# Two PSUM banks for the last token tile of the last product, and buffers of their own for an early weight tile and the last transposed tile

## The chip, the core and the metric

The kernel runs on one core of one Trainium2 chip. The metric is the device time of one execution in microseconds (us), lower is better. All inputs and the output lie in the chip's memory; nothing is kept from one execution to the next.

The engines named below are TensorE (PE: matmuls, and PEld: its weight loads), VectorE (DVE), ScalarE (ACT), GpSimd (POOL) and SyncE (SP), which here issues nearly all DMA transfers, one after the other in the order of its program.

## The reference

One post-norm encoder layer over 1024 tokens of width 1024, in fp32:

```python
x = layer_norm(ALPHA * x + hybrid_mixer(x) , ln1_g, ln1_b)      # gated spatial unit and mLSTM, then @ w_out
x = layer_norm(ALPHA * x + conv_glu_ffn(x), ln2_g, ln2_b)

def conv_glu_ffn(x, w_up, conv_w, conv_b, w_down):               # D_FF = 2816
    gate, up = split(x @ w_up)
    gate = gelu(causal_dwconv(gate, conv_w, conv_b))             # width 3
    return (gate * up) @ w_down
```

The mixer takes the first third of the time, and the change does not touch its work. The feed-forward part (`conv_glu_ffn`) and the two layer norms around it are what the text is about.

## The kernel before

**Arithmetic.** Every fp32 operand is split into a high part and a remainder (`split_hi`, L74, a cast on ACT; `split_lo`, L77, a subtraction on DVE), and every product is three matmuls (`mm3`, L304 to L306: high by high, then the two mixed ones). The split weights live in a ring of five slots, `WH0` to `WH4` and `WL0` to `WL4`; one slot holds two elements of 128x512. A slot is filled again once the matmuls that read it are done (`done_elem`, `prep`).

**The FFN's first half.** It works on 22 gate/up pairs `p`, each as seven block products (j = 0 to 6) of a Strassen-like scheme. Elements 0 and 1 of a pair are its raw gate tile, elements 2 to 5 are sums that DVE forms (`sums`, L152 to L155), element 6 is raw again. The raw tiles come into the buffer `RW` by `load_up` (L147), one DMA of 512 KB for each half, `w_up[p, 0]` to columns 0 to 1023 and `w_up[p, 1]` to the rest. Elements 0 and 1 of the first three pairs (`first_products`) need only the first half of the tokens and are done ahead, while the mixer's last stage still runs.

**The hand-over from mixer to FFN.** The out-projection goes over eight token tiles t = 0 to 7 (`proj`, matmul L701). For each tile DVE adds the residual (L801) and takes the statistics (L713), centres (L729), and scales (L731, the last step of LN1); SP stores the tile to memory (L803, `x1d`); PE transposes it (`x1T`, L748), ACT copies the transposed halves from PSUM (L749) back over the tile in `acc[t]`, and DVE forms operand sums from it (L760 to L763). `XOP` and `TX` name the resulting operands. Tile 7 is the last; the FFN's operands for the second half of the tokens need it.

**The FFN's second half** (`down_all`) is again a set of seven products, P2, P1, P5, P6, P3, P7, P4 in that order, each of 11 chunks `c` and, for each chunk, four token tiles. Chunk c of the j-th product is step s = 11 j + c, so the last product P4 has s = 66 to 76. Its weight operands are also prepared through the ring (`prep_t`: a load L174, a subtraction L194, and the split). The result of a product and token tile is collected in one bank of PSUM, TensorE's output memory (`A`, four banks named `mm` in the trace; `C`, four named `sm`). `take` (L925, L927) adds a bank to the output tile `acc`.

**What orders the work.** The order of the instructions on each engine is set by a scheduler when the program is built, from the order of the code and the dependences, except in the last product: `down_end` is written under `manual_schedule`, so its order is that of the code. There, before, chunks 0 to 2 of P4 are done for all four token tiles (`HEAD = 3`), then chunks 3 to 10 for tile 0, 1 and 2 of the second half one after the other (acc 4, 5, 6), and then for the last one (acc 7) in two halves of 256 columns. Both halves lie in the same bank, `C[3]`. Behind each, DVE adds (L987; L998 for the last tile's halves) and takes statistics, and `centre`, `affine` (L939, L940) do LN2.

Of the kernel before, what the change touches and what calls it, by code (L numbers as in the profile page):

```python
# [35 lines left out]
def hybrid_encoder_layer(ctx, tc, xT, x, w_qk, w_vg, w_au, w_av, w_o, w_out, w_up, w_down,  # L36
# [100 lines left out]

    def raw_of(p, j, n=1):
        if j in (0, 1):
            return RW[:, j * 512:(j + n) * 512]  # L140
        if j == 6:
            return RW[:, 1536:2048]
        return AP_[0][:, (j - 2) * 512:(j - 2 + n) * 512]
# [10 lines left out]
        nc.vector.tensor_tensor(s3, a11, a21, op=ALU.subtract)  # L154
        nc.vector.tensor_tensor(s4, a12, s2, op=ALU.subtract)  # L155

    def runs(s):

        if s >= 7 * NC:
            return []  # L160
        if s == 7 * NC - 1:
            return [(s, 1)]
        return [(s, 2)] if s // NC == (s + 1) // NC else [(s, 1), (s + 1, 1)]


# [10 lines left out]
    def prep_t(s, n):  # L176

        nonlocal ntr
        name, c = PRODS[s // NC], s % NC
        ch = chain[0][:, c * 512:(c + n) * 512] if chain else None  # L180
        if name == "P1":
            raw = ch
        else:
            raw = TR[ntr % 4][:, 0:n * 512]
            ntr += 1
        load_t(raw.rearrange("p (c d) -> p c d", c=n), name, c, n)
        if name in ("P5", "P6", "P7", "P4"):
            if name in ("P5", "P6"):
                nc.vector.tensor_tensor(ch, raw, ch, op=ALU.subtract)
                raw = ch  # L190
            elif name == "P7":
                nc.vector.tensor_tensor(raw, ch, raw, op=ALU.subtract)
            else:
                nc.vector.tensor_tensor(raw, raw, ch, op=ALU.subtract)  # L194
        split(E1 + s, raw, n)

    chain = []

# [5 lines left out]
    def prep(e):  # L204

        if e >= E1:
            for s, n in runs(e - E1):
                prep_t(s, n)
            return
        i = e - E0  # L210
        two = SEQ[i:i + 2]
        if i == 0:
            load_up(0)
        if two[0][0] == two[1][0] and two[0][1] in (0, 2, 3, 4):
            p, j = two[0]
            if j == 2 and p > 0:
                sums(p)
            split(e, raw_of(p, j, 2), 2)
            if j == 0 and 0 < p < EARLY - 1:
                load_up(p + 1, (0,))  # L220
            return
        for q, (p, j) in enumerate(two):
            if j == 2 and p > 0:
                sums(p)
            split(e + q, raw_of(p, j))
            if j == 6 and p + 1 < NF:
                load_up(p + 1)
# [512 lines left out]
    def x1T(t):  # L740

        ts_ = slice((t % 4) * P, (t % 4 + 1) * P)
        a3 = acc[t].rearrange("p (k t) -> p k t", k=NK)
        for g in range(2):
            pt = smps()
            for i in range(4):
                k = g * 4 + i
                nc.tensor.transpose(pt[:, i * P:(i + 1) * P], acc[t][:, k * P:(k + 1) * P], ident)  # L748
            nc.scalar.copy(acc[t][:, g * 512:(g + 1) * 512], pt)  # L749

        def put(xh, xl, src):
            split_hi(xh[:, :, ts_], src)
            split_lo(xl[:, :, ts_], src, xh[:, :, ts_])

        if t < 4:
            put(XH[0], XL[0], a3)
            return
        b3 = acc[t - 4].rearrange("p (k t) -> p k t", k=NK)
        t3 = tmp.tile([P, 512], F32, name="t2", bufs=4).rearrange("p (k t) -> p k t", k=4)
        nc.vector.tensor_tensor(t3, a3[:, 4:8, :], a3[:, 0:4, :], op=ALU.subtract)  # L760
        nc.vector.tensor_tensor(a3[:, 0:4, :], a3[:, 0:4, :], b3[:, 0:4, :], op=ALU.subtract)
        nc.vector.tensor_tensor(b3[:, 0:4, :], a3[:, 4:8, :], a3[:, 0:4, :], op=ALU.subtract)
        nc.vector.tensor_tensor(b3[:, 4:8, :], b3[:, 4:8, :], b3[:, 0:4, :], op=ALU.subtract)  # L763
        late_puts["TX"].append(lambda: put(*TX24, b3))
        late_puts["X1"].append(lambda: put(XH[1], XL[1], a3))
        late_puts["T3"].append(lambda: put(*XOP["T3"], t3))
# [7 lines left out]
    for t in range(NT):  # L774
        nc.sync.dma_start(acc[t], x[t * P:(t + 1) * P, :])
        pss = [mmps(), mmps()]
        if t == NT - 1:
            sums(0)
            load_up(1, (0,))
        proj(t, ys, pss, range(4))  # L780
        nys = prep_y(t + 1) if t < NT - 1 else None
        if t == NT - 2:
            mctx.close()
            fctx = ExitStack()
            ffn = fctx.enter_context(tc.tile_pool(name="ffn", bufs=1, reuse_waits="tile"))
            TX24 = [ffn.tile([P, NK, 512], F32R, name=f"TX{i}") for i in range(2)]
            GR2 = ffn.tile([P, 1032], F32, name="GR2")
            XOP.update(T2=[w[:, 0:4, :] for w in TX24], T4=[w[:, 4:8, :] for w in TX24],
                       T3=(JJ.rearrange("p (k t) -> p k t", k=4), T3L))
        if t >= NT - 2:  # L790
            puts("TX")
        proj(t, ys, pss, (4, 5))
        if t >= 1:
            x1T(t - 1)
        if t >= NT - 2:
            puts("TX")
        proj(t, ys, pss, (6, 7))
        ys = nys
        for g in range(2):
            a = acc[t][:, g * 512:(g + 1) * 512]  # L800
            nc.vector.scalar_tensor_tensor(a, a, ALPHA, pss[g], op0=ALU.mult, op1=ALU.add)  # L801
        ln_dve(acc[t], lng, moments(stats(acc[t], HALVES)))
        nc.sync.dma_start(x1d[t], acc[t])  # L803
# [82 lines left out]
    def load_s(s0):  # L886

        nonlocal nsr
        for s, n in runs(s0):
            raw = SR[nsr % len(SR)][:, 0:n * 512].rearrange("p (c t) -> p c t", c=n)  # L890
            nsr += 1
            nc.sync.dma_start(raw, sd[s // NC, s % NC:s % NC + n].rearrange("c p t -> p c t"))
            sh, sl = s_slot(s, n)
            split_hi(sh, raw)
            split_lo(sl, raw, sh)

    def step(j, c, bank, t, first, cols=slice(0, 512)):
        s, tail = j * NC + c, j == len(PRODS) - 1
        th, tl = elem(E1 + s)
        sh, sl = (w[:, 0, t * P:(t + 1) * P] for w in s_slot(s, 1))  # L900
        mm3(bank[:, cols], sh, sl, th[:, cols], tl[:, cols], first and c == 0, c == NC - 1 or tail and c == HEAD - 1,
            not first or tail and c >= HEAD)

    def done_step(j, c):
        s = j * NC + c
        done_elem(E1 + s)
        if s % 2 == 1:
            load_s(s + 15)

    HEAD = 3  # L910

    def down_product(name, bank, first, between=None):
        j = PRODS.index(name)
        for c in range(NC if name != "P4" else HEAD):
            if c == 4 and between:
                between()
            for t in range(4):
                step(j, c, bank[t], t, first)
            done_step(j, c)

# [54 lines left out]
    def down_end(A, C):  # L975
        j = PRODS.index("P4")
        take(A, 1, 1, False)
        down_product("P4", C, True)
        half_stats(1, 1)
        take(A, 1, 0, True)  # L980
        for t in range(3):
            for c in range(HEAD, NC):
                step(j, c, C[t], t, True)
            if t == 2:
                affine(5, nc.gpsimd, nc.sync)
            a = acc[4 + t][:, 0:512]
            nc.vector.tensor_tensor(a, a, C[t], op=ALU.add)  # L987
            nc.vector.bn_stats(LS[:, 4 + t, 0, :], a)
            centre(4 + t)
            if t == 1:  # L990
                affine(4, nc.gpsimd, nc.sync)
        t, a = NT - 1, acc[NT - 1]
        for i, cols in enumerate((slice(0, 256), slice(256, 512))):
            for c in range(HEAD, NC):
                step(j, c, C[3], 3, True, cols)
            if i == 0:
                affine(6, nc.vector, nc.sync)
            nc.vector.tensor_tensor(a[:, cols], a[:, cols], C[3][:, cols], op=ALU.add)  # L998
            nc.vector.bn_stats(LS[:, t, 2 * i, :], a[:, cols])
        mv = moments_of(t, 3)  # L1000
        rs = rstd_of(mv[:, 1:2], 1)
        nc.vector.scalar_tensor_tensor(a, a, mv[:, 0:1], lng[0], op0=ALU.subtract, op1=ALU.mult)
        for (lo, hi), q in zip(((0, 512), (512, 1024)), (nc.scalar, nc.sync)):
            nc.vector.scalar_tensor_tensor(a[:, lo:hi], a[:, lo:hi], rs, lng[1][:, lo:hi], op0=ALU.mult, op1=ALU.add)
            q.dma_start(out[t * P:(t + 1) * P, lo:hi], a[:, lo:hi])
# [83 lines left out]
```

## Time and profile before

| what | value |
|---|---|
| time, median of 3 runs | 1035.51 us (1035.13 to 1036.37) |
| the profiled execution: its own time | 1035.04 us |
| its span on the engines | 1033.2 us |
| mean granted clock of TensorE | 0.993 of full speed |
| busy: PE / PEld | 1013.2 us (98%) / 827.9 us (80%) |
| busy: DVE / ACT / POOL | 695.7 us (67%) / 428.6 us (41%) / 72.2 us (7%) |

The span runs from the first to the last instruction that the profiler saw; the profiled execution's own time is 1.84 us more (1035.04 - 1033.2). All times of rows below are counted from the start of the span. Busy shares are means over the span: what a wait costs has to be read where it is.

### The profile page before, as it was taken

Reading aid. Unit: us, or ns where it says so; the run is one execution under the profiler, and the core shown is the slowest. Engines: PE = TensorE matmul, PEld = TensorE weight load, DVE = VectorE, ACT = ScalarE, POOL = GpSimd, SP = SyncE. Lnnn points to the kernel's source line nnn. Section 1 sums busy time; section 2 is a strip of 40 time slices with the busy share of each in tenths; the row PEclk is TensorE's granted clock in tenths of the full one; section 3 lists DMA queues with packets and bytes.
Section 4 is the critical chain, followed back from the end, with each engine's and each line's share of the span. In section 5 each row is a group of like instructions: output and inputs, shape, how many; then the busy total and the mean of one; then the engine's idle time right before and its main releaser. Section 6 shows DMA issues by size and latency. Waiting matters only on the chain.

```text
span 1033.2 us, 12796 instructions
## 1 busy us (share of the span) xinstructions
PE 1013.2 (98%) x4769; PEld 827.9 (80%) x4769; DVE 695.7 (67%) x1187; ACT 428.6 (41%) x659; POOL 72.2 (7%) x84
## 2 busy tenths in 40 slices
PE   9999999999999989999999999999999999999994
PEld 7899777888888867888888888888888888888884
DVE  7432346775566789877776776776776688466885
ACT  6533666342222245443343443443345453333410
POOL 0000112222100000000000000000000000000512
PEclk9999999999999999999999999999999999999997
DMA  8122420333111142332322322322346998256312
GB/s 291 61 71 82 124 82 22 114 111 102 62 62 42 41 158 90 131 111 82 130 95 82 126 99 82 122 102 82 119 168 223 318 311 284 104 174 203 133 51 82
DMA packets 60254, 127.32 MB, mean 123 GB/s; under 512 B 6624, under 2 KB 8992, under 8 KB 60192
## 3 DMA queue, kind: packets, MB, share of 16 engines
q1 hardware_dynamic: 60048, 126.24, 36.3%
q8 instruction: 37, 0.61, 0.2%
q10 hardware_dynamic: 144, 0.26, 0.1%
q14 instruction: 25, 0.20, 0.1%
HBM read 97.88 MB, written 28.61 MB: 122 GB/s over the span
## 4 chain that ended last, share of the span: by engine, by line
PE 60%; DVE 3%; DMA 0%; POOL 0%; ACT 0%; issue 0%; POOLq 0%; DVEq 0%
PE mm L305 15%; PE mm L306 15%; PE mm L304 15%; PE sm L304 6%; PE sm L306 6%; PE sm L305 6%; DMA RW<-in_w_up_dram 0%; DVE WL L77 0%; DVE ACC L939 0%; DVE ACC L731 0%; ACT ACC L734 0%; POOL rs L296 0%; POOL ACC L940 0%; POOLq L1085 0%; DVE t L760 0%
## 5 line engine op out<-in xcount | busy, mean ns | idle before, releaser
L304 PE MATMUL mm<-XH,WH 128*128 128x512 f32 x392 | 156.2, 398 | 3.0 <-ACT WH L74 2.5
L305 PE MATMUL mm<-XL,WH 128*128 128x512 f32 x392 | 155.0, 395 | 1.0 <-DVE XL L77 1.0
L306 PE MATMUL mm<-XH,WL 128*128 128x512 f32 x392 | 155.4, 397 | 0.0
L77 DVE TENSOR_TENSOR WL<-RW,WH 128x512 fp32r<-128x512 f32 (+3 forms) x115 | 95.1, 834 | 52.8 <-ACT WH L74 51.2
L74 ACT CAST WH<-RW 128x512 fp32r<-128x512 f32 (+3 forms) x115 | 79.7, 699 | 122.0 <-PE mm L305 55.1
L304 PEld LDWEIGHTS mm<-XH,WH 128*128 128x128 f32 x392 | 74.1, 189 | 21.3 <-ACT WH L74 3.5
L305 PEld LDWEIGHTS mm<-XL,WH 128*128 128x128 f32 x392 | 74.1, 189 | 18.9 <-DVE XL L77 2.0
L306 PEld LDWEIGHTS mm<-XH,WL 128*128 128x128 f32 x392 | 73.9, 188 | 18.0 <-DVE WL L77 1.1
L296 POOL TENSOR_TENSOR rs<-ve,negh 128x4 f32<-128x4 f32 (+1 forms) x32 | 29.4, 922 | 765.0 <-DVE ve L294 762.0
L304 PE MATMUL sm<-WH,XH 128*128 128x512 f32 (+1 forms) x184 | 71.9, 391 | 6.6 <-DVE ACC L998 6.6
L347 PE MATMUL mm<-WH,XH 128*128 128x260 f32 (+1 forms) x256 | 77.3, 342 | 0.0
L347 PE MATMUL mm<-WH,XL 128*128 128x260 f32 (+1 forms) x256 | 76.2, 338 | 0.0
L347 PE MATMUL mm<-WL,XH 128*128 128x260 f32 (+1 forms) x256 | 76.1, 338 | 0.0
L74 ACT CAST XH<-SR 128x1024 fp32r<-128x1024 f32 (+1 forms) x38 | 36.8, 971 | 89.7 <-PE mm L305 45.8
L74 ACT CAST WH<-AP 128x1024 fp32r<-128x1024 f32 (+1 forms) x55 | 48.2, 879 | 58.4 <-PE mm L305 25.8
L305 PE MATMUL sm<-WL,XH 128*128 128x512 f32 (+1 forms) x184 | 71.7, 390 | 0.0
L306 PE MATMUL sm<-WH,XL 128*128 128x512 f32 (+1 forms) x184 | 71.6, 389 | 0.0
L304 PE MATMUL mm<-TX,WH 128*128 128x512 f32 x176 | 69.4, 394 | 0.0
L305 PE MATMUL mm<-TX,WH 128*128 128x512 f32 x176 | 69.3, 394 | 0.0
L306 PE MATMUL mm<-TX,WL 128*128 128x512 f32 x176 | 69.2, 393 | 0.0
L77 DVE TENSOR_TENSOR XL<-SR,XH 128x1024 fp32r<-128x1024 f32 (+1 forms) x38 | 44.6, 1180 | 34.0 <-ACT XH L74 33.9
L77 DVE TENSOR_TENSOR WL<-AP,WH 128x1024 fp32r<-128x1024 f32 (+1 forms) x55 | 55.3, 1007 | 5.6 <-ACT WH L74 4.6
(273 smaller groups left out, 2043.5 us busy)
## 6 DMA issues: line engine op xcount, KB each, us to landing
RW<-in_w_up_dram SPq DMA_DIRECT2D x46, 512.0 KB, 3.4
SR<-sd SPq DMA_DIRECT2D x31, 512.0 KB, 4.2
sd<-ACC SPq DMA_DIRECT2D x44, 256.0 KB, 3.1
S<-in_w_down_dram SPq DMA_DIRECT2D x15, 512.0 KB, 4.7
RW<-in_w_down_dram SPq DMA_DIRECT2D x15, 512.0 KB, 4.6
sd<-t SPq DMA_DIRECT2D x22, 256.0 KB, 2.6
RW<-in_w_out_dram SPq DMA_DIRECT2D x16, 256.0 KB, 3.2
S<-in_xT_dram SPq DMA_DIRECT2D x12, 256.0 KB, 5.5
```

Source lines behind the costliest of these rows:

```text
L74: nc.scalar.copy(hi, src)
L77: nc.vector.tensor_tensor(lo, src, hi.bitcast(F32), op=ALU.subtract)
L296: nc.gpsimd.tensor_tensor(rs, ve, negh[:, 0:n], op=ALU.pow)
L304: nc.tensor.matmul(ps, lh, rh, start=first, stop=False, skip_group_check=more)
L305: nc.tensor.matmul(ps, lh, rl, start=False, stop=False, skip_group_check=more)
L306: nc.tensor.matmul(ps, ll, rh, start=False, stop=last, skip_group_check=more)
L347: nc.tensor.matmul(pss[g][:, 0:width], lhs[:, k, :], rhs[:, k % 2, g * width:(g + 1) * width], start=(k == 0 and i == 0), stop=(k == NK - ...
```

## The change

It has four parts. (1) The early gate tile of pair 1 is loaded to a buffer of its own, `late[3]` (named S3), and `RW` takes pair 2's at once; before, pair 2's was loaded after pair 1's had been split. (2) The transposed last tile is written to `lng[0]` (named S9), not back over `acc[7]`. (3) The operand of the very last step, s = 76, has a place of its own in `JJ`, and is prepared at the end of P7. (4) In P4, chunks 0 and 1 (`HEAD = 2`) are done for three token tiles; the last token tile comes alone afterwards with all 11 chunks, its second half in another bank (`mmps()`), and `affine(6)` on DVE stands behind the first half's add.

```diff
     def raw_of(p, j, n=1):
         if j in (0, 1):
-            return RW[:, j * 512:(j + n) * 512]
+            return (late[3] if p == 1 else RW)[:, j * 512:(j + n) * 512]
...
-    def runs(s):
+    def runs(s, left=False):
...
         if s == 7 * NC - 1:
-            return [(s, 1)]
+            return [(s, 1)] if left else []
...
-        split(E1 + s, raw, n)
+        wh, wl = t_op(s, n)
+        split_hi(wh, raw)
+        split_lo(wl, raw, wh)
+
+    def t_op(s, n=1):
+        return (JJ[:, 0:512], JJ[:, 512:1024]) if s == 7 * NC - 1 else elem(E1 + s, n)
...
             split(e, raw_of(p, j, 2), 2)
-            if j == 0 and 0 < p < EARLY - 1:
-                load_up(p + 1, (0,))
...
-        a3 = acc[t].rearrange("p (k t) -> p k t", k=NK)
+        raw = acc[t] if t < NT - 1 else lng[0]
+        a3 = raw.rearrange("p (k t) -> p k t", k=NK)
...
-            nc.scalar.copy(acc[t][:, g * 512:(g + 1) * 512], pt)
+            nc.scalar.copy(raw[:, g * 512:(g + 1) * 512], pt)
...
         if t == NT - 1:
+            nc.sync.dma_start(late[3][:, 0:1024], w_up[1, 0])
             sums(0)
-            load_up(1, (0,))
+            load_up(2, (0,))
...
-        s, tail = j * NC + c, j == len(PRODS) - 1
-        th, tl = elem(E1 + s)
+        s = j * NC + c
+        th, tl = t_op(s)
...
         done_elem(E1 + s)
+        if s == 6 * NC - 1:
+            prep_t(7 * NC - 1, 1)
...
-    HEAD = 3
+    HEAD = 2
...
-            for t in range(4):
+            for t in range(4 if name != "P4" else 3):
                 step(j, c, bank[t], t, first)
...
-        for i, cols in enumerate((slice(0, 256), slice(256, 512))):
-            for c in range(HEAD, NC):
-                step(j, c, C[3], 3, True, cols)
-            if i == 0:
+        for i, (cols, bank) in enumerate(((slice(0, 256), C[3]), (slice(256, 512), mmps()))):
+            for c in range(NC):
+                step(j, c, bank, 3, True, cols)
+            if i == 1:
                 affine(6, nc.vector, nc.sync)
-            nc.vector.tensor_tensor(a[:, cols], a[:, cols], C[3][:, cols], op=ALU.add)
+            nc.vector.tensor_tensor(a[:, cols], a[:, cols], bank[:, cols], op=ALU.add)
```

`load_up(1)`, later in the program, is unchanged and brings `w_up[1, 0]` to `RW` once more, although `S3` holds it.

In the orders below a row is one instruction: its line, its operation, what it writes, what it reads, and the size; "x2" is two in a row. SP's queue at the hand-over, before (RW is the weight buffer, x1d the store of an LN1 tile, ACC4 to ACC7 the tiles 4 to 7, S9 and S10 buffers for the second half's weights):

```order
L803 DMA x1d_945<-ACC4_83 128x1024
L803 DMA x1d_945<-ACC5_84 128x1024
L803 DMA x1d_945<-ACC6_85 128x1024
L147 DMA RW_80<-in_w_up_dram 128x1024 x2
L174 DMA S9_89<-in_w_down_dram 128x2x512
L147 DMA RW_80<-in_w_up_dram 128x1024
L803 DMA x1d_945<-ACC7_86 128x1024
L174 DMA S10_90<-in_w_down_dram 128x2x512
L147 DMA RW_80<-in_w_up_dram 128x1024 x4
```

The same place of SP's queue after the change:

```order
L808 DMA x1d_945<-ACC4_83 128x1024
L782 DMA S3_88<-in_w_up_dram 128x1024
L808 DMA x1d_945<-ACC5_84 128x1024
L808 DMA x1d_945<-ACC6_85 128x1024
L147 DMA RW_80<-in_w_up_dram 128x1024 x3
L808 DMA x1d_945<-ACC7_86 128x1024
L174 DMA S10_90<-in_w_down_dram 128x2x512
L147 DMA RW_80<-in_w_up_dram 128x1024
L174 DMA S9_89<-in_w_down_dram 128x2x512
L147 DMA RW_80<-in_w_up_dram 128x1024 x2
```

One load more stands there, S3's; the two of RW behind the store of ACC6 have become three (pair 2's gate tile, pair 1's again, pair 2's again), the S9 load has moved behind the store of ACC7, and the second half of pair 1 (the single RW load) is now behind that store and S10's load, where before it was ahead of the store.

DVE around the start of the last product, before (RW, S10 hold raw operands of the last product, `chain` the matrix that is subtracted, WL2 to WL4 ring slots, ACC4 to ACC7 the output tiles):

```order
L194 TENSOR_TENSOR RW_80<-RW_80,chain_6144 128x1024
L77 TENSOR_TENSOR WL2_77<-S10_90,WH2_72 128x1024
L927 TENSOR_TENSOR ACC4_83<-ACC4_83,mm_6165 128x512
L927 TENSOR_TENSOR ACC5_84<-ACC5_84,mm_6166 128x512
L927 TENSOR_TENSOR ACC6_85<-ACC6_85,mm_6167 128x512
L927 TENSOR_TENSOR ACC7_86<-ACC7_86,mm_6168 128x512
L194 TENSOR_TENSOR RW_80<-RW_80,chain_6144 128x512
L77 TENSOR_TENSOR WL3_78<-RW_80,WH3_73 128x1024
L77 TENSOR_TENSOR WL4_79<-RW_80,WH4_74 128x512
L931 BN_STATS LS_6147<-ACC4_83 128x6
```

The same place after the change (JJ holds the operand of step 76):

```order
L194 TENSOR_TENSOR RW_80<-RW_80,chain_6144 128x1024
L194 TENSOR_TENSOR RW_80<-RW_80,chain_6144 128x512
L77 TENSOR_TENSOR WL2_77<-S10_90,WH2_72 128x1024
L77 TENSOR_TENSOR JJ_87<-RW_80,JJ_87 128x512
L933 TENSOR_TENSOR ACC4_83<-ACC4_83,mm_6165 128x512
L933 TENSOR_TENSOR ACC5_84<-ACC5_84,mm_6166 128x512
L933 TENSOR_TENSOR ACC6_85<-ACC6_85,mm_6167 128x512
L933 TENSOR_TENSOR ACC7_86<-ACC7_86,mm_6168 128x512
L937 BN_STATS LS_6147<-ACC4_83 128x6
L77 TENSOR_TENSOR WL3_78<-RW_80,WH3_73 128x1024
L937 BN_STATS LS_6147<-ACC5_84 128x6
```

The subtraction and the split of step 76 (128x512) have moved ahead of the four adds, and the split of steps 74 and 75 (WL3) now has one statistics instruction more ahead of it.

DVE at the end, before (ACC6 and ACC7 are the last two output tiles, LN0 and LN1 the gain and bias of LN2, sm_7294 the bank of the last tile):

```order
L939 TENSOR_TENSOR ACC6_85<-ACC6_85,LN0_6145 128x1024
L940 TENSOR_TENSOR ACC6_85<-ACC6_85,LN1_6146 128x1024
L998 TENSOR_TENSOR ACC7_86<-ACC7_86,sm_7294 128x256
L999 BN_STATS LS_6147<-ACC7_86 128x6
L998 TENSOR_TENSOR ACC7_86<-ACC7_86,sm_7294 128x256
```

And after, where the last tile's halves are in sm_7298 and mm_7451:

```order
L1004 TENSOR_TENSOR ACC7_86<-ACC7_86,sm_7298 128x256
L1005 BN_STATS LS_6147<-ACC7_86 128x6
L945 TENSOR_TENSOR ACC6_85<-ACC6_85,LN0_6145 128x1024
L946 TENSOR_TENSOR ACC6_85<-ACC6_85,LN1_6146 128x1024
L1004 TENSOR_TENSOR ACC7_86<-ACC7_86,mm_7451 128x256
```

The first half's add and statistics have moved ahead of tile 6's gain and bias, and the second half's add reads another bank.

## Rows read from the trace of the kernel before

**Rows 1.** The page's first line.
```profile
span 1033.2 us, 12796 instructions
```

**Rows 2.** Waits of PE: line, what it waited for, total us, times, longest.
```profile
PE sm L304 <- DVE ACC L998: 6.6, 1, 6.6
```

**Rows 3.** Windows: us, busy time (count) by engine, granted clock, DMA share, GB/s.
```profile
377.00:377.50 0.50, 0.50 (x1) 0.48 (x2) 0.50 (x1) 0.50 (x1) 0.00 (x0) 0.50 0.56 184
389.00:389.50 0.50, 0.00 (x0) 0.00 (x0) 0.50 (x2) 0.50 (x2) 0.00 (x0) 1.00 0.00 0
440.00:980.00 540.00, 540.00 (x2333) 437.69 (x2332) 389.67 (x508) 229.20 (x304) 12.83 (x7) 1.00 0.44 150
```

**Rows 4.** PE's timeline at the hand-over: start, us, instruction, idle before and releaser.
```profile
376.98 0.79 PE L304 MATMUL mm<-XH,WH 128*128 128x512 f32 x1 [2.12 <-ACT WH L74]
...
380.47 0.39 PE L305 MATMUL mm<-XL,WH 128*128 128x512 f32 x1
...
382.39 1.06 PE L748 MATMUL sm<-ident,ACC 128*128 128x128 f32 x8 [0.59 <-DVE ACC L731]
...
389.53 0.49 PE L304 MATMUL mm<-XH,WH 128*128 128x512 f32 x1 [0.54 <-ACT XH L74]
390.80 0.50 PE L305 MATMUL mm<-XL,WH 128*128 128x512 f32 x1 [0.77 <-DVE XL L77]
...
393.74 0.49 PE L305 MATMUL mm<-TX,WH 128*128 128x512 f32 x1
```

**Rows 5.** ACT's timeline at the hand-over.
```profile
375.89 1.04 ACT L74 CAST WH<-RW 128x1024 fp32r<-128x1024 f32 x1 [2.87 <-DMA RW<-in_w_up_dram]
...
385.31 1.07 ACT L749 COPY ACC<-sm 128x512 f32<-128x512 f32 x2 [2.84 <-DMA x1d<-ACC]
...
389.39 0.61 ACT L74 CAST WH<-RW 128x512 fp32r<-128x512 f32 x1
```

**Rows 6.** DVE's timeline at the hand-over.
```profile
361.94 1.28 DVE L731 SCALAR_TENSOR_TENSOR ACC<-ACC,rs,S 128x1024 f32<-128x1024 f32 x1 [0.43 <-POOL rs L296]
...
369.62 1.23 DVE L77 TENSOR_TENSOR WL<-RW,WH 128x1024 fp32r<-128x1024 f32 x1
...
380.96 1.28 DVE L731 SCALAR_TENSOR_TENSOR ACC<-ACC,rs,S 128x1024 f32<-128x1024 f32 x1 [0.44 <-POOL ACC L811]
```

**Rows 7.** SP's queue at the hand-over, two loads of RW in one row.
```profile
364.45 6.76 SPq L147 DMA_DIRECT2D RW<-in_w_up_dram  x2
```

**Rows 8.** The tile RW from 340 to 420 us: its DMAs from issue to landing.
```profile
DMA to landing us min/median/max: 3.2/3.4/5.0
```

**Rows 9.** PE's timeline in the last product.
```profile
985.75 0.40 PE L304 MATMUL sm<-WH,XH 128*128 128x512 f32 x1
...
1010.80 0.28 PE L304 MATMUL sm<-WH,XH 128*128 128x256 f32 x1
...
1020.35 0.58 PE L304 MATMUL sm<-WH,XH 128*128 128x256 f32 x1 [6.56 <-DVE ACC L998]
```

**Rows 10.** DVE's timeline in the last product.
```profile
988.00 1.21 DVE L194 TENSOR_TENSOR RW<-RW,chain 128x1024 f32<-128x1024 f32 x1
...
990.47 2.47 DVE L927 TENSOR_TENSOR ACC<-ACC,mm 128x512 f32<-128x512 f32 x4
992.87 0.68 DVE L194 TENSOR_TENSOR RW<-RW,chain 128x512 f32<-128x512 f32 x1
...
1005.43 0.69 DVE L987 TENSOR_TENSOR ACC<-ACC,sm 128x512 f32<-128x512 f32 x1 [2.67 <-PE sm L306]
...
1017.47 1.23 DVE L939 TENSOR_TENSOR ACC<-ACC,LN 128x1024 f32<-128x1024 f32 x1 [1.31 <-ACT ACC L734]
...
1025.78 0.42 DVE L998 TENSOR_TENSOR ACC<-ACC,sm 128x256 f32<-128x256 f32 x1 [5.03 <-PE sm L306]
```

**Rows 11.** SP's queue at the end: the load of step 76's operand.
```profile
984.58 0.37 SPq L174 DMA_DIRECT2D RW<-in_w_down_dram  x1
```

**Rows 12.** DMA issues from 960 us on: engine, operation, KB each, median us to landing.
```profile
RW<-in_w_down_dram SPq DMA_DIRECT2D x1, 256.0 KB, 3.6
```

More of the change, by code (lines that the diff above doesn't have):

```diff
@@ L888, in load_s @@
         nonlocal nsr
-        for s, n in runs(s0):
+        for s, n in runs(s0, True):
             raw = SR[nsr % len(SR)][:, 0:n * 512].rearrange("p (c t) -> p c t", c=n)
@@ L897, in step @@
     def step(j, c, bank, t, first, cols=slice(0, 512)):
-        s, tail = j * NC + c, j == len(PRODS) - 1
-        th, tl = elem(E1 + s)
+        s = j * NC + c
+        th, tl = t_op(s)
         sh, sl = (w[:, 0, t * P:(t + 1) * P] for w in s_slot(s, 1))
-        mm3(bank[:, cols], sh, sl, th[:, cols], tl[:, cols], first and c == 0, c == NC - 1 or tail and c == HEAD - 1,
-            not first or tail and c >= HEAD)
+        mm3(bank[:, cols], sh, sl, th[:, cols], tl[:, cols], first and c == 0, c == NC - 1, not first)
     def done_step(j, c):
```

## The prediction, made before the changed kernel was run

> **What bounds the kernel now.** First the busy times by engine (the table above): PE is busy for 1013.2 of the 1033.2 us [rows 1], so a gain has to come from the 20 us in which it waits or from time in which it runs slowly. Then PE's waits, of which the largest is one of 6.6 us for DVE's add at L998 [rows 2]. Then the windows: from 440 to 980 us PE is busy for all 540.00 us at the full clock [rows 3], so nothing that only hastens another engine there is worth anything, and what is gained ahead of it is carried unchanged to the end. The two places to look at are the hand-over, 360 to 394 us, and the last product, from 985.75 us on.
>
> At the **hand-over** PE waits 2.12 us until 376.98 for an ACT cast of RW, and that cast starts at 375.89, when a load of RW has landed [rows 4, 5]. This is pair 2's gate tile: its load is the second of SP's row that starts at 364.45, held back until DVE's split of pair 1 at 369.62 has ended, 370.85 [rows 6, 7]. Behind the wait PE's clock is half: 0.50 in the window at 377 us against 1.00 later [rows 3], the lower of its two levels, 1.2 against 2.4 GHz. The seven starts from 376.98 to 380.47 take 3.49 us; at full clock a matmul of 512 columns takes 0.232 us in a row ((1010.80 - 985.75) / 108 matmuls between the two [rows 9]), so 1.62, and 1.87 are lost. Three short waits follow: 0.59 for tile 7's LN1 scale on DVE, then 0.54 and 0.77 for its operands [rows 4]. In all 2.12 + 1.87 + 0.59 + 0.54 + 0.77 = 5.89 us.
>
> In the **last product** the last tile's first half ends at 1020.35 - 6.56 = 1013.79, and PE does not start the second before DVE has added the first, because both are in one bank [rows 9]. DVE does not come to that add because tile 6's gain and bias (L939 at 1017.47, L940 after it) stand ahead, and they wait for ACT's normalising of tile 6 [rows 10]. The second half's add then comes at 1025.78, after 5.03 us of idle DVE, and 7.42 us of tail follow up to 1033.2.
>
> **The end, part by part.** The matmuls are as many as before: 36 + 72 of 512 columns and 24 + 24 halves against 18 + 81 and 33 + 33, 132 times 512 columns either way. What moves:
>
> (a) The second half has its own bank and follows the first at once. Its bank is one of the four that P7 used and DVE's second `take` empties; that is done about 1000, 14 us before it is wanted, so I cost it at nothing.
>
> (b) On DVE the 76-step's subtraction (0.60, a half-width instruction like the one at 992.87 [rows 10], less the 0.08 by which neighbours overlap) and its split (0.60) now stand ahead of WL2 and of the four adds, and WL3's split comes after the adds and one statistics instruction. From 988.00: subtraction 1.13, step 76's 0.60, WL2 1.14, JJ 0.60, four adds 2.40 (2.47 in a row [rows 10]), statistics 0.60, and WL3 1.22 gives 995.7. PE wants WL3 (steps 74 and 75) with the 38th matmul: tile 0 now follows after 18 matmuls of the head, not 36, and 18 more for its chunks 2 to 7, and one with the high part: 985.75 + 37 x 0.232 = 994.3. So a new wait of about 1.4. Before, 36 + 15 + 1 matmuls stood ahead, PE came to it at 997.8, and there was no wait. Below nothing it cannot be; above, it grows with any lateness of DVE.
>
> (c) The load of step 76's operand (issued at 984.58 [rows 11], 3.6 to land [rows 12]) is there at 988.2, and DVE comes to it at 989.1. It is hidden by 0.9; beyond that each us of lateness goes to PE.
>
> (d) Where that 1.4 is found again. Tile 0's end is hidden, since DVE is busy with the adds till about 1000. Tile 1 ends after 18 + 54 matmuls and the wait, 985.75 + 72 x 0.232 + 1.4 = 1003.9, and DVE's add of it starts about 1004.0; before, it started at 1005.43, after 36 + 48 = 84 matmuls and a wait for PE [rows 10]. So this add comes about 1.35 earlier. The chain behind it on DVE and ACT, 12.04 us from 1005.43 to L939's start for tile 6 at 1017.47 [rows 10], is the same instructions and bounded by their own durations: L939 of tile 6 at 1016.1. The first half's add now stands before it, in the idle 1.31 there (PE ends that half about 1014.2: 99 x 0.232 + 33 x 0.116 + 1.4 behind 985.75 is 1013.9, and the add about 1014.8). L939 and L940 take 2.4, so DVE is free for the second half's add at 1018.5. PE ends that half at 1013.9 + 33 x 0.116 = 1017.7 to 1018.1. The add at 1018.53 instead of 1025.78: a gain of **7.25**, with DVE, not PE, last. Without the wait in (b) the whole chain is 1.35 earlier still, but PE then needs 1016.7: 8.6 at most.
>
> **The hand-over.** Pair 1's gate tile is now loaded to S3 behind the store of tile 4, ahead of the loads of RW, and its split no longer has to wait for the sums of pair 0, nor to end before RW is loaded again. RW's load of pair 2 is issued once DVE has formed the sums of pair 0 and is landed by 371.6 even at the longest landing of 5.0 [rows 8]; the split is done by 373. PE wants it at 374.86. So the wait of 2.12 and the slow clock behind it, 3.99, go.
>
> What is late next is tile 7's LN1 on DVE. Two splits now stand ahead of tile 6's scale (361.94 [rows 6]), which waits 0.43 there: 361.94 + 2 x 1.14 - 0.43 = 363.8. From it to tile 7's there are, in the new order, ten instructions of half width at 0.60, five splits or centrings at 1.14 to 1.2, tile 6's own 1.2 and a small one, 13.2: about 377.2, against 380.96 before, where DVE too sat idle for the missing cast. The transposes follow 1.4 behind, about 378.6. PE, without its wait, is there at 382.39 - 0.59 - 3.99 = 377.8. A new wait of 0.8, then, and tile 7's transposes 3.8 earlier. ACT's copies of them no longer wait for the store of tile 7: before they waited 2.84 for it [rows 5], and PE was 0.54 and 0.77 late behind them [rows 4]; those 1.31 go as well. PE alone would be 3.8 + 1.31, with the early matmul below 5.4, earlier.
>
> But the other half of pair 1 (`w_up[1, 1]`) now stands in SP's queue behind the store of tile 7 and S10's load, and waits for the split of pair 0's last element, done about 382. It lands 3.2 to 5.0 later [rows 8]; with the 3.4 of the median and a little for the neighbours, at 385.7. ACT's cast of it and, behind it, three more (0.61 + 1.04 + 1.04 + 0.61 [rows 5], 3.2 with their overlaps), and DVE's sums, are queued behind that landing; with 0.3 from the last cast to PE, the matmul that stood at 393.74 [rows 4] comes 3.5 after it, at 389.2. One matmul of its group is done ahead of it, so the gain is 393.74 - 389.2 + 0.23 = **4.8**. With a landing in 5.0 it is 3.4 (387.1 instead of 385.7); it cannot be above 5.4.
>
> The load that brings `w_up[1, 0]` a second time, and pair 2's tile after it, lie in SP's queue ahead of tile 7's store and are through by 376.4, before the store can go at 378.6; they cost nothing as long as that cover of 2 us holds. The DMA engines are busy for 0.56 of the window at 377 us, with 184 GB/s [rows 3]. The Trainium skill (DMA: Bandwidth & Descriptors, "Issuing engines are not separate DMA queues") says that all transfers end on the same 16 engines and interleave; by that rule the three added or moved 512 KB loads lengthen each other, and the gain is the 3.4, the time 1024.9. Nothing in the median of the landings speaks for that, so the sum stays with 4.8.
>
> **Sum.** 1035.04 - 7.25 - 4.8 = 1023.0 for an execution like the profiled one. Its 1035.04 is 0.47 below the median of the runs, 1035.51, so I predict 1023.5, a gain of 12.0, or 1.2%. A difference within 0.2% (2.1 us) is about what a measurement of this kernel can't tell from none.
>
> **The rivals.**
> - *Hand-over gain given back.* The moved load of `w_up[1, 1]` lands late, or DVE's order makes tile 7's scale later than 377.2; the gain there is 1 to 3. For it: three loads and a store follow each other closely. Against: landings were 5.0 at most [rows 8]. Time 1025.3 to 1027.3. Chance 0.2.
> - *The clock falls in a new wait.* In the 2.12 us wait it fell, and 1.87 were lost in the matmuls after it [rows 4]; across the waits of 0.54 and 0.77, close together, it stayed at 1.00 [rows 3]. The new waits, 0.8 at the transposes and 1.4 in the last product, lie between. If it falls once, about 1.9 more: 1025.4. Chance 0.14. The Trainium skill (TensorE: Matmul & The Clock Gate, "A second HAM failure mode: psum-queue depth-cycling") reports that short idles between groups of matmuls let the clock swing; by that rule a fall is likelier than I make it.
> - *The second bank does not help*, because its emptying is late or DVE's order still holds PE. The end then keeps its 6.6 wait: 1035.5 - 4.8 = 1030.7. Chance 0.02.
> - *Slower than before.* DVE's new subtraction waits for step 76's load; DVE and then PE stand behind it. To undo 12.0 us it must be 12.9 later than 988.2, so land 16.5 us after issue, where 3.6 was measured [rows 12]. Chance 0.02; a landing that leaves the time the same (13 to 16 us), 0.02.
> - The forecast, 1021.5 to 1024.7: 0.6.
>
> **How the numbers follow.** The low end is 7.25 + 1.35 for no wait at WL3, with 5.4 at the hand-over: 1035.51 - 14.0 = 1021.5. The high end is both gains short: 7.25 - 1.9 for a fallen clock and 3.2: 1027.0. Faster by over 0.2% is all but the last cases, 0.96.
>
> **What the changed profile should show.** No wait of 6.6 us in the last tile; PE without gaps there. A wait of about 1.4 us on a DVE split about 8.5 us after the last product starts. The last half's add about 7 us nearer to the product's start, right behind L946, with 7.4 of tail. At the hand-over no wait for a cast of RW at pair 2's first element and a clock of 1.00 after it; the transposes of tile 7 some 3.8 us earlier, behind a wait of under 1 us for the scale; one wait of under 1.5 us at the first sums of pair 1, for ACT or DVE behind the load. From there to the last product everything earlier by 4.8. Wrong would be: a clock of 0.50 behind one of the new waits; WL3's wait absent or above 2; the load of `w_up[1, 1]` landing after 386.5; or PE, not DVE, last at the second half's add.

## The result and the profile after

The changed kernel takes 1022.91 us (median of 4 runs, 1022.7 to 1023.92) against 1035.32 for the kernel before in the same comparison (4 runs, 1034.93 to 1036.37): a ratio of 0.9881, 95% interval 0.9863 to 0.9898. 1023.5 was predicted. The profiled execution of after took 1022.7 us, its span is 1020.9, 12.3 less than before [rows 1].

The page's first lines of after, the span and the busy times by engine:

```profile
span 1020.9 us, 12811 instructions
...
PE 1008.1 (99%) x4778; PEld 825.1 (81%) x4778; DVE 694.3 (68%) x1187; ACT 428.6 (42%) x659; POOL 71.9 (7%) x84
```

PE's waits of after (line, waited for, total us, times, longest), beside [rows 2]:

```profile
PE sm L752 <- DVE ACC L734: 1.4, 1, 1.4
PE sm L308 <- DVE WL L77: 1.2, 1, 1.2
PE sm L248 <- DVE mrow L412: 1.1, 1, 1.1
PE mm L307 <- ACT WH L74: 1.0, 3, 0.7
```

The wait of 6.6 us is gone. The two that matter now are where they were looked for: the one at tile 7's transposes (L752), which was 0.59 before [rows 4], and a new one at the split of steps 74 and 75 (WL, L77). PE's busy time fell too, from 1013.2 to 1008.1 us, for the same amount of matmul work: mostly the matmuls that ran at half clock before.

To tell the two places apart, a span's own start has to be taken out: in the runs below, the first 20 us differ by up to 1.5 us from run to run. I count from tile 5's transposes, PE's work up to there being the same. They start, before and after:

```profile
350.15 1.08 PE L748 MATMUL sm<-ident,ACC 128*128 128x128 f32 x8
```
```profile
349.92 1.17 PE L752 MATMUL sm<-ident,ACC 128*128 128x128 f32 x8
```

PE of after at the hand-over and at the start of the last product, beside [rows 4] and [rows 9]:

```profile
376.90 0.40 PE L309 MATMUL mm<-XH,WL 128*128 128x512 f32 x1
378.73 1.06 PE L752 MATMUL sm<-ident,ACC 128*128 128x128 f32 x8 [1.43 <-DVE ACC L734]
...
388.52 0.50 PE L307 MATMUL mm<-TX,WH 128*128 128x512 f32 x1 [0.18 <-ACT WH L74]
388.86 0.39 PE L308 MATMUL mm<-TX,WH 128*128 128x512 f32 x1
...
980.54 0.40 PE L307 MATMUL sm<-WH,XH 128*128 128x512 f32 x1
...
990.52 0.50 PE L308 MATMUL sm<-WL,XH 128*128 128x512 f32 x1 [1.24 <-DVE WL L77]
```

From tile 5's transposes to the last product's start it is 980.54 - 349.92 = 630.62 us; before it was 985.75 - 350.15 = 635.60. So the hand-over gave **4.98**. The clock there (window: us, busy by engine, granted clock, DMA share, GB/s), beside [rows 3], stays at the upper level behind the wait of 1.43, and so it does behind the one of 1.24:

```profile
378.80:379.80 1.00, 1.00 (x9) 1.00 (x10) 1.00 (x2) 0.41 (x1) 0.00 (x0) 1.00 0.50 201
990.60:991.60 1.00, 1.00 (x5) 0.82 (x6) 1.00 (x3) 0.00 (x0) 0.00 (x0) 1.00 0.00 0
```

What the predicted chain hangs on, tile 7's scale on DVE, SP's queue, and the landing of `w_up[1, 1]` as ACT sees it:

```profile
377.30 1.28 DVE L734 SCALAR_TENSOR_TENSOR ACC<-ACC,rs,S 128x1024 f32<-128x1024 f32 x1 [0.44 <-POOL rs L299]
```
```profile
366.23 10.26 SPq L147 DMA_DIRECT2D RW<-in_w_up_dram  x3
378.61 0.33 SPq L808 DMA_DIRECT2D x1d<-ACC  x1
...
382.08 0.34 SPq L147 DMA_DIRECT2D RW<-in_w_up_dram  x1
```
```profile
379.39 1.07 ACT L753 COPY S<-sm 128x512 f32<-128x512 f32 x2 [0.97 <-PE sm L752]
...
385.29 0.62 ACT L74 CAST WH<-RW 128x512 fp32r<-128x512 f32 x1 [1.50 <-DMA RW<-in_w_up_dram]
```

The scale starts at 377.30 (377.2 predicted); the copies of the transposes no longer wait for a store; the load is issued at 382.08 and there at 385.29 (382 and 385.7).

DVE of after in the last product, beside [rows 10]:

```profile
989.27 1.20 DVE L77 TENSOR_TENSOR WL<-RW,WH 128x1024 fp32r<-128x1024 f32 x1
...
998.96 0.69 DVE L993 TENSOR_TENSOR ACC<-ACC,sm 128x512 f32<-128x512 f32 x1 [1.62 <-PE sm L309]
...
1009.66 0.41 DVE L1004 TENSOR_TENSOR ACC<-ACC,sm 128x256 f32<-128x256 f32 x1
...
1012.31 1.23 DVE L946 TENSOR_TENSOR ACC<-ACC,LN 128x1024 f32<-128x1024 f32 x1
1013.46 0.41 DVE L1004 TENSOR_TENSOR ACC<-ACC,mm 128x256 f32<-128x256 f32 x1
```

From the last product's start to the last add: 1013.46 - 980.54 = 32.92 us, before 1025.78 - 985.75 = 40.03, a gain of **7.11**. The last add stands right behind L946, without a wait for PE, whose last matmul starts at 1012.68. 4.98 + 7.11, with 0.23 from the start (350.15 - 349.92), make the 12.3.

### The profile page after: what moved, and what is told of

Same layout as the page of the kernel before. It is cut to its first block, busy times and chain, and to the rows that moved or that the text cites. A ratio compares the mean times of both kernels' runs of the same rounds, so it can differ in the third digit from the quotient of the medians.

```text
span 1020.9 us, 12811 instructions
## 1 busy us (share of the span) xinstructions
PE 1008.1 (99%) x4778; PEld 825.1 (81%) x4778; DVE 694.3 (68%) x1187; ACT 428.6 (42%) x659; POOL 71.9 (7%) x84
## 4 chain that ended last, share of the span: by engine, by line
PE 90%; DVE 6%; POOL 1%; issue 1%; ACT 0%; DMA 0%; POOLq 0%; SPq 0%; DVEq 0%
PE mm L307 17%; PE mm L309 17%; PE mm L308 16%; PE mm L350 13%; PE mm L704 8%; PE sm L308 5%; PE sm L309 5%; PE sm L307 5%; DVE WL L77 1%; PE mm L522 1%; DVE XL L77 1%; POOL rs L299 1%; PE sm L603 1%; PE mm L525 1%; PE sm L752 1%
## 5 line engine op out<-in xcount | busy, mean ns | idle before, releaser
L308 PE MATMUL mm<-XL,WH 128*128 128x512 f32 x392 | 154.3, 394 | 0.0
L77 DVE TENSOR_TENSOR WL<-RW,WH 128x512 fp32r<-128x512 f32 (+3 forms) x113 | 93.3, 830 | 55.9 <-ACT WH L74 54.3
L308 PEld LDWEIGHTS mm<-XL,WH 128*128 128x128 f32 x392 | 73.7, 188 | 17.4 <-DVE XL L77 0.6
L308 PE MATMUL mm<-TX,WH 128*128 128x512 f32 x176 | 69.2, 393 | 0.0
L308 PE MATMUL sm<-WL,XH 128*128 128x512 f32 (+1 forms) x172 | 66.7, 388 | 1.2 <-DVE WL L77 1.2
L77 DVE TENSOR_TENSOR XL<-SR,XH 128x1024 fp32r<-128x1024 f32 (+1 forms) x38 | 44.6, 1180 | 33.2 <-ACT XH L74 33.1
L307 PE MATMUL sm<-WH,XH 128*128 128x512 f32 (+1 forms) x172 | 66.7, 388 | 0.0
L309 PE MATMUL sm<-WH,XL 128*128 128x512 f32 (+1 forms) x172 | 66.6, 387 | 0.0
L77 DVE TENSOR_TENSOR WL<-AP,WH 128x1024 fp32r<-128x1024 f32 (+1 forms) x55 | 55.3, 1007 | 5.8 <-ACT WH L74 4.8
```

The costliest lines, as they stand in the source:

```text
L77: nc.vector.tensor_tensor(lo, src, hi.bitcast(F32), op=ALU.subtract)
L307: nc.tensor.matmul(ps, lh, rh, start=first, stop=False, skip_group_check=more)
L308: nc.tensor.matmul(ps, lh, rl, start=False, stop=False, skip_group_check=more)
L309: nc.tensor.matmul(ps, ll, rh, start=False, stop=last, skip_group_check=more)
```

## The experiments

The theory is that the change is two gains that have nothing to do with each other: at the hand-over, the late gate tile with its slow clock, and tile 7's operands; at the end, one long wait of PE that comes from a shared bank and an order on DVE together. The rivals: that one of the two edits at each place does it all, that the gains are not independent, and, for what is left, that the new waits can or can't be had back. In the table, "hand-over" is the time from tile 5's transposes to the last product's start, "end" from there to the last add, both read from one profiled execution as above; the ratio is to the kernel before, timed beside it on the same chip.

| run | median us | ratio (95%) | hand-over | end |
|---|---|---|---|---|
| before | 1035.32 | 1 | 635.60 | 40.03 |
| after | 1022.91 | 0.9881 (0.9863 to 0.9898) | 630.62 | 32.92 |
| e1 hand-over only | 1029.88 | 0.9954 (0.9942 to 0.9967) | 630.55 | 39.39 |
| e2 end only | 1028.69 | 0.9941 (0.9929 to 0.9954) | 635.50 | 32.91 |
| e3 early gate only | 1034.85 | 0.9998 (0.9989 to 1.0007) | 633.85 | 39.42 |
| e4 own tile 7 only | 1032.97 | 0.9985 (0.9976 to 0.9994) | 633.88 | 40.13 |
| e5 one bank | 1023.86 | 0.9895 (0.9882 to 0.9909) | 630.57 | 33.76 |
| e6 affine first | 1023.60 | 0.9893 (0.9879 to 0.9906) | 630.55 | 33.69 |
| e7 both | 1029.60 | 0.9950 (0.9936 to 0.9963) | 630.52 | 40.18 |
| e8 before, affine second | 1030.33 | 0.9956 (0.9943 to 0.9968) | 635.88 | 35.43 |
| e9 WL3 first | 1021.51 | 0.9875 (0.9860 to 0.9889) | 630.53 | 31.46 |
| e10 head of 3 | 1022.29 | 0.9880 (0.9864 to 0.9897) | 630.48 | 32.17 |
| e11 LN first | 1022.63 | 0.9884 (0.9869 to 0.9899) | 630.51 | 32.90 |
| e12 e9, no reload | 1022.28 | 0.9872 (0.9856 to 0.9888) | 630.63 | 31.72 |

The kernel before was 1034.70 beside e1 to e4, 1034.85 beside e5 to e8, 1034.63 beside e9 to e11 and 1036.18 beside e12; ratios compare across these, medians do so less well. How far one execution can be trusted shows in the runs that share a place: the seven with the hand-over as in after take 630.48 to 630.62 there, the three with it as in before (before, e2, e8) 635.50 to 635.88. The end takes 32.90 to 32.92 where it is as in after (after, e2, e11), but 39.39 to 40.13 where it is as in before (before, e1, e3, e4).

**e1, the hand-over's two parts alone** (the kernel before with the diff's lines on `raw_of`, `load_up`, `late[3]` and `lng[0]`, nothing else):

> The kernel before with the first two parts alone (pair 1's early gate tile in S3, the last transposed tile in S9). Theory: the two halves of the change are independent, because PE has no gap between them; the last product starts 5.2 us earlier (985.75 to 980.5) and the rest is as before: 1035.3 - 5.2 = 1030.1 us, with the 6.6 us wait for L998's add still there. Rival (the hand-over's gain is lost again when the end is not changed, or needs it): above 1032.

**e2, the end's two parts alone** (the diff's other lines):

> The kernel before with the last two parts alone (step 76's own place, head of two chunks, last tile alone in two banks). Theory: from the last product's start to the last add 7.1 us less, hand-over unchanged: 1035.3 - 7.1 = 1028.2 us, so that this and the other half's gain add up to 12.3. Rival: the two overlap, and the sum of the separate gains is above or below 12.3 by more than 1.

1029.88 and 1028.69. e1's hand-over is after's to 0.07 us, e2's end to 0.01, and each has the other place as before: in the traces the gains are independent. The medians can't show it so well: e1 and e2 lie 4.8 and 6.0 us below the kernel before, 10.8 together, which is more than 1 below the 12.3 of the expectation and so on the rival's side; by the ratios it is 0.46% and 0.59% against 1.19%, and the intervals are too wide to tell these apart. (e1's end is 0.64 shorter than before's though its long wait is the same 6.5: PE's clock came back within the last half tile there.)

**e3, the early gate tile alone**, and **e4, the own place of the last transposed tile alone.** e3 is e1 without

```diff
-        raw = acc[t] if t < NT - 1 else lng[0]
-            nc.scalar.copy(raw[:, g * 512:(g + 1) * 512], pt)
+            nc.scalar.copy(acc[t][:, g * 512:(g + 1) * 512], pt)
```

and e4 is the kernel before with those lines alone.

> The kernel before with the first part alone; the last transposed tile goes back over acc[7], so ACT's copies wait for the store of tile 7 again. Theory: that store lands about 381.6 (issued 378.6, 3.0 to land), the copies start 2.3 us later than the 379.39 they have with a buffer of their own, of which 0.3 is slack and the rest is a wait of PE: of the 5.2 us 3.2 remain: 1032.1 us. Rival (the store is no bound, the own buffer is worth nothing): 1030.1.

> The kernel before with the second part alone. Theory: the wait of 2.12 us for pair 2's gate tile and the slow matmuls behind it stay; of the three short waits after them the 0.54 and 0.77 go: 1035.3 - 1.3 = 1034.0 us. Rival (what counts there is the load of pair 1's other half, which now stands behind the store of tile 7): no gain, 1035.3 or more.

e3's hand-over is 1.75 shorter, not 3.2, and its time can't be told from that of before: by the interval it gains 1.1 us at most. The trace is of one of its better executions. The three of eleven with the highest mean granted clock, 0.994, the profiled one among them, took 1032.57 to 1033.69 us, and the eight at 0.993 and 0.991 took 1034.21 to 1036.65; where those lost their time no trace shows. PE in e3 has the wait at the transposes and two more at the hand-over:

```profile
PE mm L302 <- ACT TX L74: 1.8, 1, 1.8
PE mm L302 <- ACT XH L74: 1.5, 1, 1.5
PE sm L746 <- DVE ACC L729: 1.4, 1, 1.4
```

ACT's copies of tile 7 in e3 wait 4.09 us for the store:

```profile
383.69 1.07 ACT L747 COPY ACC<-sm 128x512 f32<-128x512 f32 x2 [4.09 <-DMA x1d<-ACC]
```

Against after, whose tile 5 stands 1.26 earlier in its span (349.92 against 351.18), the copies are 383.69 - 379.39 - 1.26 = 3.04 later, not 2.3 (the store took 3.9 from its issue at 379.78), and the hand-over is 633.85 - 630.62 = 3.23 longer. The slack of 0.3 that I had allowed is not there. e4's 1.72 is near the 1.3 expected. 1.75 + 1.72 = 3.47 is less than the 4.98 of both together: the early gate tile puts PE ahead of tile 7's operands, and the store then holds these, so each part alone leaves a wait that the other removes.

**e5 to e7, the end's bank and order undone, one by one and together.** The edits to the changed kernel, e5 the first, e6 the second, e7 both:

```diff
-        for i, (cols, bank) in enumerate(((slice(0, 256), C[3]), (slice(256, 512), mmps()))):
+        for i, (cols, bank) in enumerate(((slice(0, 256), C[3]), (slice(256, 512), C[3]))):
...
-            if i == 1:
+            if i == 0:
                 affine(6, nc.vector, nc.sync)
```

> The changed kernel with both halves of the last tile in one bank, C[3]; tile 6's gain and bias stay behind the first half's add. Theory (it is the long wait that costs, and either of the two edits removes it): PE's second half starts behind the first half's add, 1010.1 instead of 1008.9, and the last add comes about 0.9 us later: 1022.9 + 0.9 = 1023.8. Rival (the second bank is what gains): the wait of some 5 us is back, 1028 or more.

> The changed kernel with tile 6's gain and bias ahead of the first half's add again; two banks stay. Theory: PE waits for nothing, DVE has the first half's add and statistics (0.84 us) between L946 and the last add, so the last add is 0.84 later: 1023.7. Rival (the order on DVE is what gains): 1026 or more.

> The changed kernel with both undone: one bank, and tile 6's gain and bias ahead of the first half's add; head of two chunks and step 76's place stay. Theory: PE waits from 1009.0 to the add at 1013.5 to 1013.9, 4.8 us, and its 33 half matmuls then run in 3.9 us at full clock or 7.7 at half: the last add 4.4 to 8.3 us later, 1027.3 to 1031.2. Rival (each edit is worth its own 0.9 and no more): 1024.6.

Each alone costs 0.8 us at the end (33.76 and 33.69 against 32.92), both together 7.26. The 0.8 is the traces': the ratios of e5 and e6 overlap after's. e7's end is no shorter than before's (40.18 and 40.03), so without the bank and the order nothing of the gain is left; that step 76's own place or the head of two chunks gains anything by itself is not shown. PE's waits for the first half's add, in e5 and in e7:

```profile
PE sm L307 <- DVE ACC L1004: 1.1, 1, 1.1
```
```profile
PE sm L307 <- DVE ACC L1004: 4.9, 1, 4.9
```

In e7 the second half's 33 matmuls take from 1013.86 to the last start at 1020.37, 6.5 us, where after has them in 3.8 (1008.90 to 1012.68); the clock of e7 shows why:

```profile
1013.86 0.58 PE L307 MATMUL sm<-WH,XH 128*128 128x256 f32 x1 [4.85 <-DVE ACC L1004]
...
1020.37 0.28 PE L309 MATMUL sm<-JJ,XL 128*128 128x256 f32 x1
```
```profile
1014.50:1015.50 1.00, 1.00 (x6) 1.00 (x6) 0.00 (x0) 0.00 (x0) 0.00 (x0) 0.50 1.01 418
1016.00:1017.00 1.00, 1.00 (x6) 1.00 (x6) 0.00 (x0) 0.00 (x0) 0.00 (x0) 0.50 0.00 0
```

So about 2.7 of the 7.26 are the half clock behind the wait, and the rest the later start of the second half (1013.86 against 1008.90, less the half microsecond by which DVE is last in after).

**e8, one line of the kernel before moved**, `if i == 0:` to `if i == 1:` ahead of `affine(6, ...)`, one bank, everything else as before:

> The kernel before with one line changed: tile 6's gain and bias stand behind the first half's add (the second half's loop pass), everything else as before, one bank. Theory: the first half's add comes at 1016.1 instead of 1019.88, PE waits 2.8 us instead of 6.6, and the last add is 3.4 us earlier if the clock falls in that wait as before, 5.9 if it doesn't: 1029.4 to 1031.9. Rival (the gain needs the second bank): 1035.3.

1030.33, and 4.60 of the end's 7.11 with no second bank. PE waits 2.8 us and not 6.6; the clock falls after that wait too, but later:

```profile
1017.20:1018.00 0.80, 0.80 (x8) 0.80 (x9) 0.28 (x2) 0.73 (x1) 0.00 (x0) 1.00 1.00 404
1018.00:1018.50 0.50, 0.50 (x5) 0.50 (x5) 0.50 (x1) 0.00 (x0) 0.00 (x0) 0.64 0.11 41
1018.50:1019.50 1.00, 1.00 (x6) 1.00 (x6) 0.97 (x2) 0.00 (x0) 0.00 (x0) 0.50 0.00 0
```

**e9, the split of steps 74 and 75 ahead of the adds** (the changed kernel; it is prepared in `down_end` and no longer by `done_elem`):

```diff
-        done_elem(E1 + s)
         if s == 6 * NC - 1:
             prep_t(7 * NC - 1, 1)
+        else:
+            done_elem(E1 + s)
...
+        prep_t(7 * NC - 3, 2)
         take(A, 1, 1, False)
```

> The changed kernel with the split of steps 74 and 75 (slot WL3) prepared ahead of the four adds that empty P7's banks. Theory (the new wait of 1.24 us is DVE's order alone, and DVE's chain behind tile 1 is what ends last): WL3 is done near 987.5 and not 990.5, the wait goes, the four adds are 1.13 later where DVE has room, and everything from tile 1's add on is 1.2 us earlier: 1022.9 - 1.2 = 1021.7. Rival (the chain behind DVE's adds of the other tiles is last): no change, 1022.9.

**e10, `HEAD = 3`** for the three token tiles of the changed kernel:

> The changed kernel with a head of three chunks for the three token tiles. Theory: 42 matmuls and not 36 stand ahead of the first that needs WL3, PE comes to it at about 990.5 when it is ready, so PE loses nothing and ends 1.2 us earlier; but tile 1's last matmul has three more ahead of it (0.7 us), so its add, and the chain on DVE behind it up to the last add, is only 0.5 earlier: 1022.4. Rival (PE is last at the end): 1021.7.

DVE's WL3 and the last add, in e9 and in e10:

```profile
986.89 1.22 DVE L77 TENSOR_TENSOR WL<-RW,WH 128x1024 fp32r<-128x1024 f32 x1
...
1012.34 0.41 DVE L1006 TENSOR_TENSOR ACC<-ACC,mm 128x256 f32<-128x256 f32 x1
```
```profile
989.64 1.20 DVE L77 TENSOR_TENSOR WL<-RW,WH 128x1024 fp32r<-128x1024 f32 x1
...
1013.10 0.41 DVE L1004 TENSOR_TENSOR ACC<-ACC,mm 128x256 f32<-128x256 f32 x1
```

The wait at WL3 is gone from PE in both. e9's end is 1.46 shorter than after's, e10's 0.75. In e10 PE's last matmul starts at 1011.63, 30.70 behind the last product's start, and in after 32.14: PE gained 1.44, and the end only half of it, as much as tile 1's add on DVE (998.62 - 980.93 = 17.69 behind the last product's start, in after 998.96 - 980.54 = 18.42). So DVE, by way of tile 1's add, is last in after, as predicted, and in the traces the change's head of two chunks costs 0.75 against one of three. e9's 1021.51 is the lowest median here; its ratio and after's overlap, so the runs alone do not separate the two, the traces do.

**e11, LN1 with priority** (`with tc.high_priority():` around the residual add and `ln_dve` of each tile, in the changed kernel):

> The changed kernel with LN1 of every token tile (residual add, statistics, centring, scale) given priority over other work when the order is made. Tile 7's scale then stands some six instructions earlier on DVE, its transposes earlier on PE, and its store earlier in SP's queue; the sums of pair 0, and so pair 2's gate load, come later. Theory (tile 7's scale is what the hand-over still waits for): the 1.43 us wait at its transposes goes, 1021.5. Rival (the load of pair 1's other half and what is queued behind it is last anyway): the wait is found again at the first sums of pair 1, 1022.5 to 1022.9. Second rival: pair 2's gate tile is late again and the wait for it is back, 1023.5 or more.

1022.63, as the first rival had it. PE in e11 reaches the transposes five microseconds earlier in its order with nearly no wait, and waits at pair 1's first sums instead (0.28 and 1.18, in after 1.43 and 0.18):

```profile
373.28 1.06 PE L752 MATMUL sm<-ident,ACC 128*128 128x128 f32 x8 [0.28 <-DVE ACC L734]
...
393.61 0.50 PE L307 MATMUL mm<-TX,WH 128*128 128x512 f32 x1 [1.18 <-ACT WH L74]
```

The hand-over takes 630.51 us, against 630.62. ACT there waits for the load of `w_up[1, 1]`, and this one is issued late, at 387.12, behind the split of pair 0's last element, which the new order put later on DVE:

```profile
386.41 0.68 DVE L77 TENSOR_TENSOR WL<-RW,WH 128x512 fp32r<-128x512 f32 x1
```
```profile
387.12 13.01 SPq L147 DMA_DIRECT2D RW<-in_w_up_dram  x3
```
```profile
390.33 0.62 ACT L74 CAST WH<-RW 128x512 fp32r<-128x512 f32 x1 [1.79 <-DMA RW<-in_w_up_dram]
```

So earlier transposes with that load later gave nothing; the load is last. As e11 made the load five microseconds later as well, it does not tell what earlier transposes would give with the load where it was. In after PE waits 0.18 for a cast behind that load at 388.52, so without an earlier load it could be little.

**e12, e9 without the second loads** of `w_up[1, 0]` and `w_up[2, 0]`:

```diff
-                load_up(p + 1)
+                load_up(p + 1, (1,) if p + 1 in (1, 2) else (0, 1))
```

> The changed kernel with WL3's split ahead of the adds (as in the run before) and without the two loads of 512 KB that bring w_up[1, 0] and w_up[2, 0] to RW a second time. Theory (those loads lie in SP's queue where it would wait for tile 7's store anyway): the hand-over from tile 5's transposes to the last product's start stays at 630.5 us, 1021.5 in all. Rival (all transfers share the DMA engines, and without these two the load of w_up[1, 1] lands earlier): 0.2 to 0.5 us less.

The hand-over stays at 630.63. The load of `w_up[1, 1]` is used 3.4 us after its issue, with the reloads (after) 3.2:

```profile
382.42 0.34 SPq L147 DMA_DIRECT2D RW<-in_w_up_dram  x1
```
```profile
385.84 0.62 ACT L74 CAST WH<-RW 128x512 fp32r<-128x512 f32 x1 [1.75 <-DMA RW<-in_w_up_dram]
```

So the reloads cost nothing that shows in the traces, and the ratios of e9 and e12 agree. (The end of e12 is 0.26 longer than e9's with the same order there, which I can't explain.)

## Why the prediction was right

**The sum.** 7.25 + 4.8 = 12.05 were predicted, 7.11 + 4.98 = 12.09 were found, by the steps that were named. That the sums agree to 0.04 is luck: 0.14 too much at the end and 0.18 too little at the hand-over cancel, and by the ends of e1 and e3 (39.39 and 39.42) in place of before's 40.03 the gain there would be 6.5 and not 7.11.

**The end.** The second bank, emptied long before, cost nothing. The new wait at WL3 was put at 1.4 and is 1.24; it was read from DVE's order, not from the change's purpose, and e9 shows that it is that order. That DVE and not PE is last at the second half's add was right (e10, and e6's 0.84 of moved add and statistics come back as 0.77). What the prediction did not say is that the gain needs only one of the two edits: it told of the bank as what stops PE and of L939 and L940 as what delays DVE, and took both away, but e5 and e6 show that either is enough for all but 0.8, and e8 that moving one line does most of it without a bank. And a part of the 7.11 is the clock: before, the second half's 24 matmuls took 1025.42 - 1020.35 = 5.1 us from first start to last, the first half's 24 at full clock 1013.50 - 1010.80 = 2.7. The row of the add at 1025.78 held that part, so the sum was right without naming it.

**The hand-over.** The wait of 2.12 and the slow matmuls behind it are gone. The wait at the transposes was put at 0.8 and is 1.43. The term that was mis-sized is PE's arrival, 377.8 predicted and 377.3 found (376.90 + 0.40): 0.23 of the difference is the span's start, and the rest a wait of before that the prediction had left out, 0.26 for the scale of tile 6, which went as well. Tile 6's transposes, before and after:

```profile
363.37 1.06 PE L748 MATMUL sm<-ident,ACC 128*128 128x128 f32 x8 [0.26 <-DVE ACC L731]
```
```profile
365.14 1.06 PE L752 MATMUL sm<-ident,ACC 128*128 128x128 f32 x8
```

Tile 7's transposes came at 378.73, as said (378.6). The longer wait cost next to nothing, because, as the prediction had it, the operands behind the landing of `w_up[1, 1]` are last: PE waits for them again, 0.18, at 388.52. The matmul that stood at 393.74 (L305 there, L308 here) starts at 388.86 in after, or 389.1 counted from before's start, where 389.2 was predicted. On the same count the landing was at 385.5 (385.29 + 0.23) and not at 385.7, which is the size of the difference from 4.8 to 4.98.

**The rivals.** The hand-over's gain was not given back. The clock stayed at its upper level behind the waits of 1.43 and 1.24. The Trainium skill (TensorE: Matmul & The Clock Gate, "A second HAM failure mode: psum-queue depth-cycling") tells of a kernel whose TensorE idled between groups of matmuls so frequently that the clock swung. Two single waits without a fall neither bear that out nor speak against it. The Trainium skill (DMA: Bandwidth & Descriptors, "Issuing engines are not separate DMA queues") has all transfers interleave on the same 16 engines. By the prediction's estimate that could cost 1.4, and no such cost is seen: the load of `w_up[1, 1]` was there 3.2 after its issue. e12 takes 1 MB of transfers away and finds no gain, but it does not test that sharing: the reloads were issued by 376.49, 5.6 us ahead of that load, and no landing of before took longer than 5.0 [rows 8]. Step 76's load did not hold DVE: its subtraction follows the one before it without a gap.

**What stays open.** Why e3's store took 3.9 us and not 3.0 wasn't tried, nor why most of e3's executions gained nothing. Step 76's own place was not undone by itself. Nor was an earlier load of `w_up[1, 1]` tried together with earlier transposes, which by e11 is the next thing at the hand-over.

## What to carry to other kernels

A long wait often has two conditions, here a shared bank and an order on the engine that empties it; taking away either one may give nearly all the gain, and the cheaper one is found only by undoing them singly as well as together. Before a wait is costed away, ask what is next behind it on the same path: both new waits and the last engine of each place could be read from the order and the durations of before. When two profiled executions are compared, count from a common instruction behind the start-up.

## What the hardware showed that was not expected

The clock does not always fall with the wait. In the kernel before it was at 0.50 from the first matmul behind its 2.12 us wait [rows 3]. In e8 PE waited 2.76 us and started again at 1017.03 with the clock at 1.00; it fell about a microsecond later (0.64 in the window from 1018.0 to 1018.5, 0.50 after it). In e4, which has the wait of before at the hand-over (2.34 there, until 377.68), it was still at 1.00 from 377.7 to 378.7 and at 0.50 from 380.0 to 381.0. It also came back at different times in the last half tile, behind waits of 6.56 us in before and 6.54 in e1: in before only as its last matmul ran, in e1 for the last seven. Before, and e1:

```profile
1024.50:1025.50 1.00, 1.00 (x7) 1.00 (x5) 0.00 (x0) 0.00 (x0) 0.00 (x0) 0.50 0.00 0
```
```profile
1018.00:1019.00 1.00, 1.00 (x9) 1.00 (x7) 0.00 (x0) 0.00 (x0) 0.00 (x0) 0.69 0.00 0
```

Their ends differ by 0.64 us. So of a wait that lowers the clock the length can be read from one execution; the price behind it, in these rows, only to about that 0.6.
